# adaLN rows paced anew beside the second FFN matrix, activations split ahead of it, five plain blocks for seven in the last FFN

## The chip, the cores and the metric

One core of a Trainium2 chip. The metric is the device time of one execution in microseconds (us), the median of the runs shown. Everything is fp32; a product is made on TensorE from operands split into a high and a low part (hi·hi + hi·lo + lo·hi), so each product is three matmuls, and every weight that is loaded must first be split: ScalarE copies the rounded high part, VectorE subtracts it to get the low part.

## What is computed

Two layers; each is FFN half-step, mixer, FFN half-step, on 640 tokens (128 context, 512 latent). The rows `mod` (adaLN) are one vector-matrix product per conditioning vector (two of them) and per kind of row:

```python
def adaln(cvec, w_mod_l, b_mod_l):
    m = jax.nn.silu(cvec) @ w_mod_l + b_mod_l
    return m.reshape(cvec.shape[0], N_MOD, D_MODEL)

def swiglu(h, w1, w2):
    g, u = jnp.split(h @ w1, 2, axis=-1)
    return (jax.nn.silu(g) * u) @ w2

def ffn_half(x, mod, j, g_pre, g_post, w1, w2):
    h = modulate(rms_norm(x, g_pre), mod, j)
    return x + 0.5 * mod[:, j + 2][:, None, :] * rms_norm(swiglu(h, w1, w2), g_post)
```

with D_MODEL 1024 and D_FF 2816, that is 22 blocks of 128.

## The kernel before, in words

There are six stages: 0, 2, 3, 5 are FFNs, 1 and 4 are mixers. Tokens are held in two groups: A (two tiles of 128, width 256) and B (three tiles, width 384; the third is the context tile, number 4).

**First matrix.** Loop over 22 blocks f of D_FF. The first N_AONLY[s] blocks are run for group A alone, while VectorE, ScalarE and GpSimd finish the previous stage's boundary (norm, modulation, transposes) for group B. Then these blocks are run for group B; all but the last KEEP_F = 2 of them load and split their weights a second time for that. In stages 2, 3 and 5 (BLOCKS) the remaining blocks f are computed by `ffn1_blocks` (L651), which forms seven products of combined operands in place of eight plain ones; beside group B's plain blocks VectorE prepares the combined activations (`sums`, L612, then `sum_in_place`, L639). A pair of weight tiles of a block is loaded into the pool `tmp`, which has four buffers.

**Second matrix.** `ffn2` (L748) runs over the 22 blocks twice: a first pass for group A (22 x 2 x 2 x 3 = 264 matmuls of 512 columns) and a second pass for group B (396). The activations are split block by block, two blocks ahead (L765, L766). Results lie in PSUM banks fixed by tile (OB): tile 0 in banks 4 and 5, tile 1 in 6 and 7, tile 4 again in banks 4 and 5, so tile 4's matmuls of the second pass need tile 0's boundary to have read its banks. `second_pass` (L1364) lets the boundary of group A run at the head of the second pass.

**adaLN rows.** `ada` (L418) makes one row set per kind (G, S or T): eight loads of 512 KB of w_mod, for each of them two VectorE products with accumulation of 128x1024 (L436), one for each conditioning vector, then four matmuls with ones (L445) and, for G and S, one VectorE combination (L451, L453); the result is written to DRAM (L457) and loaded again, spread over all partitions, by `load_md` (L460). A row set is so 16 products at L436. The work is a generator that yields its estimated cost: 8 x (300 + 2 x 1150) + 1700 = 22500 ns a row set. `run` (L122) and `beside` (L137) advance it by a rate times the cost that the matmuls yield: 22 x 2 x 2 x 650 = 57200 ns in a first pass, 85800 ns in a second.

What is made where: stage 0 makes two stages' rows beside its first matrix, and ADA_LATE says which are made beside the second matrix: rows of stage 2 (three sets) in stage 0, rows of stage 3 (three) in stage 2, rows of stages 4 and 5 (three and one, as the last stage has no next) in stage 3, none in stage 5. The rate is ADA_RATE2 = 0.7 in both passes. The loads of `ada` are issued on SP's queue, in one line with the weight loads; their three buffers come free when L436 has read them.

The framework puts the instructions of each engine into a fixed order when the program is built, from their place in the program, their dependences and a cost model; `behind` moves the rows' instructions a little back in priority.

Of the kernel before, what the change touches and what calls it, by code (L numbers as in the profile page):

```python
# [8 lines left out]
F32 = mybir.dt.float32  # L9
F32R = mybir.dt.float32r  # L10
# [5 lines left out]
P = 128  # L16
D = 1024
KD = 8
FF = 2816
NF = 22  # L20
# [5 lines left out]
WA = 256  # L26
WB = 384
NEG = -1e30
OB = {0: (4, 5), 1: (6, 7), 2: (0, 1), 3: (2, 3), 4: (4, 5)}
N_AONLY = (7, 0, 5, 5, 0, 7)  # L30
ADA_LAG = 30
ADA_RATE = 0.65

ADA_LATE = {0: (2,), 2: (3,), 3: (4, 5), 5: ()}
ADA_RATE2 = 0.7

BLOCKS = (2, 3, 5)
S_LAG, S_RATE = 400, 0.45
# [112 lines left out]
def drain(*gens):  # L151
    for g in gens:
        for _ in g:
            pass
# [7 lines left out]
class Builder:  # L162
    def __init__(self, ctx, tc, a, n_stage=6):
        self.tc = tc
        self.nc = tc.nc
        self.a = a
        self.n_stage = n_stage
        pool = lambda name, bufs, **kw: ctx.enter_context(tc.tile_pool(name=name, bufs=bufs, **kw))
        self.c1 = pool("c1", 1)
        self.rawp = pool("raw", 5)  # L170
        self.wp = pool("wsp", 8)
        self.xp = pool("xp", 3)
        self.tmpp = pool("tmp", 4)
        self.stp = pool("st", 6)
        self.mdp = pool("md", 2)
        self.psp = pool("ps", 1, space=bass.MemoryType.PSUM)
        self.PS = self.psp.tile([P, 4096], F32, name="PS")
        self.ring = {}
        self.turn = {}
        self.drp = pool("dr", 1, space=bass.MemoryType.DRAM)  # L180
        self.xd = [self.drp.tile([P, D], F32, name=f"xd{t}", tag=f"xd{t}") for t in range(NT)]
        self.units = []
        self.plan()
        self.n_dma = 0
        self.n_split = 0
        self.n_use = 0
        self.dmas = []
        self.raws = {}
        self.spl = {}
        self.kept = {}  # L190
        self.pins = []
        self.lo_pool = 0
        self.xt = {}
        self.hT = {}
        self.md = {}
        self.rowd = {}
        self.pairs = {}
        self.gap = None
        self.kept_tmp = {}

    def bank(self, i):
# [498 lines left out]
    def mm_tok(self, key, tiles, order, stat, late=0, tail=1):  # L700
# [18 lines left out]
        while ci < n:  # L719
# [25 lines left out]
                    yield 650 * len(tiles)  # L745
            ci += 1

    def ffn2(self, l, i, g, last=False):  # L748
        wid = (WA, WB)[g]
        sp = {}  # L750

        order = list(range(NF))
        if g:
# [543 lines left out]
    def ffn_stage(self, s, l, i, pend):  # L1297
# [3 lines left out]
        na = N_AONLY[s]  # L1301
# [4 lines left out]
        with tc.tile_pool(name="gap", bufs=1, reuse_waits="tile") as gp, tc.tile_pool(name="actp", bufs=1, reuse_waits="tile") as ap, ExitStack() as late:  # L1306
# [19 lines left out]
            if s in BLOCKS:  # L1326
                with tc.tile_pool(name="sp", bufs=2, reuse_waits="tile") as sp:
                    self.sp = sp
                    self.SZ = [sp.tile([P, 4, 2 * WA + P], F32R, name=f"sz{n}", bufs=1) for n in range(2)]
                    self.S1 = [self.mdp.tile([P, D], F32, name=f"s1{n}", tag="mdG").bitcast(F32R).rearrange("p (k q) -> p k q", k=4) for n in range(2)]  # L1330
                    bg = behind(tc, self.sums(), S_LAG)
                    run(self.ffn1(l, i, fk + early[:-1], (1,)), (bg, S_RATE))
                    drain(bg)
                    self.load_pair(l, i, na)
                    run(self.ffn1(l, i, early[-1:], (1,)))
                    self.sum_in_place()
                    self.rings(acc=(0, 1, 2, 3, 4, 5, 6, 7))
                    run(self.ffn1_blocks(l, i, range(na, NF)))
            if s in BLOCKS:
                pools()  # L1340
            ada = lambda rows: behind(tc, self.ada(rows, block(self.wmp, "wmt"), block(self.accsp, "acc")), ADA_LAG)
# [12 lines left out]
                self.load_md(kind, s)  # L1354
            self.rings(ada=(3,))
            bg = ada(rows[1])
            run(self.ffn2(l, i, 0), (bg, ADA_RATE2))
            self.rings(ada=(7,))
            self.second_pass(s, last, self.ffn2(l, i, 1, last), bg)
            for t in (3, 4):  # L1360
# [3 lines left out]
    def second_pass(self, s, last, mm, bg=None):  # L1364
        q = STG[s]
        if bg:
            mm = beside(mm, bg, ADA_RATE2)
        b = self.boundary(s, GA, True, not last, 1, q["skew_a"])
        next(b)
        next(b)  # L1370
# [84 lines left out]
```

## Time and profile before

| | us |
|---|---|
| median of 3 runs | 2384.79 (2383.39 to 2386.68) |
| the profiled execution, device time | 2385.23 |
| its span in the trace | 2383.5 |
| stage 0, second matrix (first pass, second pass) | 66.57, 99.63 |
| stage 2, the same | 70.01, 97.57 |
| stage 3, the same | 69.11, 99.86 |
| stage 5, the same | 59.88, 89.56 |
| TensorE busy in the span | 2300.2 (97%) |
| VectorE busy in the span | 1827.1 (77%) |

A pass begins with its first matmul on the split activations and ends where the next one's begins. TensorE's busy time counts a matmul until its modelled end, so in the matmul stretches start-to-start times say more than the busy share: a stretch without gaps starts a 512-column matmul every 0.226 us.

### The profile page before, as it was taken

To read this page: it belongs to the slowest core of one execution; us is meant where nothing else is said; L and a number is where in the kernel's file an instruction comes from. 1 tells how busy PE (TensorE), PEld (TensorE's weight loads), DVE (VectorE), ACT (ScalarE), POOL (GpSimd) and SP (SyncE) were. 2 spreads that over 40 slices of the span, in tenths; PEclk is the share of its full clock that TensorE was granted. 3 is DMA by queue.
4 is the path that set the end of the run, shared out by engine and by line. 5 is a ranking of instruction groups with operands and counts; after the bars stand their busy time and mean duration, and the time that the engine had idled before them with its cause. 6 is when DMAs were issued, how large, how long until landed. Compare 5 with 4: busy or idle time off the path is not lost.

```text
span 2383.5 us, 37305 instructions
## 1 busy us (share of the span) xinstructions
PE 2300.2 (97%) x13304; PEld 2050.9 (86%) x13304; DVE 1827.1 (77%) x2914; ACT 1118.5 (47%) x2309; POOL 393.5 (17%) x432
## 2 busy tenths in 40 slices
PE   8999999999999999998999999999999989999998
PEld 6999897787778899996789999877777779999887
DVE  5568678977686788889976888899867674888754
ACT  5422224444776344454443444444555553444543
POOL 2000000305324200000240000020645360000000
PEclk9999999999999999999999999999999999999999
DMA  9457657644325522247653322667621354232542
GB/s 295 117 174 244 200 189 261 232 157 137 98 72 168 160 85 84 80 160 248 222 181 120 89 86 75 212 227 244 204 74 63 106 173 134 75 89 71 187 158 93
DMA packets 330481, 360.07 MB, mean 151 GB/s; under 512 B 20451, under 2 KB 239843, under 8 KB 330294
## 3 DMA queue, kind: packets, MB, share of 16 engines
q1 hardware_dynamic: 326694, 344.58, 45.5%
q10 hardware_dynamic: 3600, 13.11, 1.4%
q8 instruction: 104, 1.70, 0.3%
q14 instruction: 83, 0.68, 0.1%
HBM read 341.50 MB, written 16.12 MB: 150 GB/s over the span
## 4 chain that ended last, share of the span: by engine, by line
PE 71%; DVE 13%; DMA 6%; issue 5%; POOL 2%; ACT 2%; SPq 1%; DVEq 0%; ACTq 0%; POOLq 0%
PE PS L366 69%; DVE wlo L331 3%; DMA wmt<-in_w_mod 3%; DVE acc L436 3%; DMA raw<-in_ffn_w 2%; DVE alo L766 1%; PE PS L445 1%; POOL tmp L520 1%; DVE ast L1063 1%; DVE x L509 1%; PE PS L1086 1%; DVE tl L362 1%; DVE h1lo L362 1%; POOL wlo L331 1%; ACT whi L329 0%
## 5 line engine op out<-in xcount | busy, mean ns | idle before, releaser
L329 ACT ACTIVATE whi<-raw 128x512 fp32r<-128x512 f32 x668 | 416.5, 630 | 525.5 <-PE PS L366 379.5
L331 DVE TENSOR_TENSOR wlo<-raw,whi 128x512 fp32r<-128x512 f32 x614 | 455.2, 755 | 198.7 <-ACT whi L329 190.0
L366 PE MATMUL PS<-whi,ahi 128*128 128x512 f32 x920 | 353.6, 392 | 0.0
L366 PE MATMUL PS<-h1hi,whi 128*128 128x384 f32 (+1 forms) x1016 | 341.5, 337 | 6.4 <-ACT h1hi L361 6.4
L366 PE MATMUL PS<-h1lo,whi 128*128 128x384 f32 (+1 forms) x1016 | 344.6, 339 | 0.0
L366 PE MATMUL PS<-wlo,ahi 128*128 128x512 f32 x880 | 342.7, 391 | 0.0
L366 PE MATMUL PS<-h1hi,wlo 128*128 128x384 f32 (+1 forms) x1016 | 341.8, 336 | 0.0
L329 ACT ACTIVATE whi<-tmp 128x512 fp32r<-128x512 f32 x294 | 185.7, 633 | 244.6 <-PE PS L366 175.3
L436 DVE SCALAR_TENSOR_TENSOR acc<-wmt,ccs,acc 128x1024 f32<-128x1024 f32 x224 | 279.9, 1279 | 26.8 <-DMA wmt<-in_w_mod 26.7
L366 PE MATMUL PS<-h0hi,whi 128*128 128x256 f32 x1016 | 287.3, 284 | 7.6 <-DVE act L602 7.4
L366 PE MATMUL PS<-whi,alo 128*128 128x512 f32 x840 | 272.7, 395 | 21.2 <-DVE alo L766 20.9
L366 PE MATMUL PS<-h0hi,wlo 128*128 128x256 f32 x1016 | 285.4, 282 | 0.0
L366 PE MATMUL PS<-h0lo,whi 128*128 128x256 f32 x1016 | 285.3, 281 | 0.0
L331 DVE TENSOR_TENSOR wlo<-tmp,whi 128x512 fp32r<-128x512 f32 x294 | 201.7, 687 | 77.5 <-ACT whi L329 71.4
L366 PEld LDWEIGHTS PS<-whi,alo 128*128 128x128 f32 x840 | 155.3, 188 | 66.6 <-DVE alo L766 30.0
L366 PEld LDWEIGHTS PS<-h0hi,whi 128*128 128x128 f32 x1016 | 193.5, 191 | 18.4 <-DVE act L602 8.8
L366 PEld LDWEIGHTS PS<-whi,ahi 128*128 128x128 f32 x920 | 173.8, 189 | 39.1 <-ACT ahi L765 1.7
L366 PE MATMUL PS<-sz,whi 128*128 128x384 f32 x784 | 199.3, 335 | 0.0
L366 PEld LDWEIGHTS PS<-h0hi,wlo 128*128 128x128 f32 x1016 | 193.6, 191 | 4.3 <-issue 3.4
L366 PEld LDWEIGHTS PS<-h1hi,whi 128*128 128x128 f32 x1016 | 190.7, 188 | 7.0 <-ACT h1hi L361 7.0
L366 PEld LDWEIGHTS PS<-wlo,ahi 128*128 128x128 f32 x880 | 166.2, 189 | 34.7
L366 PEld LDWEIGHTS PS<-h0lo,whi 128*128 128x128 f32 x1016 | 193.9, 191 | 1.8 <-issue 1.7
(239 smaller groups left out, 4204.6 us busy)
## 6 DMA issues: line engine op xcount, KB each, us to landing
raw<-in_ffn_w SPq DMA_DIRECT2D x540, 256.0 KB
wmt<-in_w_mod SPq DMA_DIRECT2D x136, 512.0 KB
tmp<-in_ffn_w SPq DMA_DIRECT2D x98, 512.0 KB
raw<-in_w_in SPq DMA_DIRECT2D x80, 256.0 KB
xd<-x ACTq DMA_DIRECT2D x25, 512.0 KB
x<-xd SPq DMA_DIRECT2D x25, 512.0 KB
raw<-in_w_out SPq DMA_DIRECT2D x64, 128.0 KB
mdG<-rowG SPq DMA_DIRECT2D x12, 512.0 KB
```

What stands on the lines that cost most here:

```text
L329: self.nc.scalar.activation(hi, r, AF.Copy)
L331: eng.tensor_tensor(lo, r, hi.bitcast(F32), ALU.subtract)
L362: i1 = (eng or self.nc.vector).tensor_tensor(lo, src, hi.bitcast(F32), ALU.subtract)
L366: self.nc.tensor.matmul(out, w, m, start=start, stop=stop)
L436: nc.vector.scalar_tensor_tensor(accs[s], w, self.cc[:, s, k:k + 1], prev, ALU.mult, ALU.add)
L445: nc.tensor.matmul(ps[32 * q:32 * q + 32, :], self.ones[:, 0:32], accs[q // 2][:, 512 * (q % 2):512 * (q % 2) + 512], start=True, stop=Tru ...
L509: nc.vector.scalar_tensor_tensor(x, tmp, r, x, ALU.mult, ALU.add)
L520: nc.gpsimd.tensor_tensor(tmp[:, hs], tmp[:, hs], self.md["T", st][:, hs], ALU.add)
L766: self.nc.vector.tensor_tensor(lo, a, hi[:, 0:wid].bitcast(F32), ALU.subtract)
L1063: nc.vector.tensor_reduce(mx, S, AX.X, ALU.max)
L1086: nc.tensor.transpose(ps[:, w * c + P * j:w * c + P * j + P], pt[:, n * j + P * (c0 + c):n * j + P * (c0 + c) + P], self.ident)
```

## The change

The rates become a pair for each stage (first pass, second pass): 0.3 and 0.62 in stages 0, 2 and 3, 0.5 and 0.62 in stage 5. Stage 5's one row set moves from stage 3 to stage 5's own first pass; what is left of it is issued behind that pass, and the loading of the row follows there. Before the last combined block of the first matrix the activations of blocks 0 and 1 for group A are split into one buffer of the pool `tmp`, and the first pass starts with them. In stage 5 five blocks in place of seven are plain, so two more go through `ffn1_blocks`.

```diff
-N_AONLY = (7, 0, 5, 5, 0, 7)
+N_AONLY = (7, 0, 5, 5, 0, 5)
-ADA_LATE = {0: (2,), 2: (3,), 3: (4, 5), 5: ()}
-ADA_RATE2 = 0.7
+ADA_LATE = {0: (2,), 2: (3,), 3: (4,), 5: (5,)}
+ADA_RATES = {0: (0.3, 0.62), 2: (0.3, 0.62), 3: (0.3, 0.62), 5: (0.5, 0.62)}
+    def split_first(self):
+
+        t = self.tmpp.tile([P, D], F32, name="first", tag="tmp").bitcast(F32R)
+        self.early = {}
+        for f in range(2):
+            hi, lo = (t[:, 512 * f + WA * n:512 * f + WA * n + WA] for n in range(2))
+            self.split(hi, lo, self.act[f, 0])
+            self.early[f] = (hi, lo)
     def ffn2(self, l, i, g, last=False):
         sp = {}
+        if g == 0 and self.early:
+            sp, self.early = self.early, {}
-                    run(self.ffn1_blocks(l, i, range(na, NF)))
+                    run(self.ffn1_blocks(l, i, range(na, NF - 1)))
+                    self.split_first()
+                    run(self.ffn1_blocks(l, i, range(NF - 1, NF)))
-            run(self.ffn2(l, i, 0), (bg, ADA_RATE2))
+            run(self.ffn2(l, i, 0), (bg, ADA_RATES[s][0]))
+            if last:
+                drain(bg)
+                self.load_md("G", s)
     def second_pass(self, s, last, mm, bg=None):
-            mm = beside(mm, bg, ADA_RATE2)
+            mm = beside(mm, bg, ADA_RATES[s][1])
```

## Rows read from the trace of the kernel before

**Rows 1.** Windows, eight passes: busy (xcount) of PE, PEld, DVE, ACT, POOL; PEclk, DMA share, GB/s.
```profile
364.30:430.87 66.57, 63.26 (x274) 49.42 (x273) 60.05 (x84) 30.29 (x58) 0.95 (x1) 1.00 0.79 261
430.87:530.50 99.63, 97.08 (x429) 77.14 (x428) 82.43 (x105) 46.53 (x88) 20.05 (x16) 0.98 0.56 185
1054.37:1124.38 70.01, 63.48 (x273) 49.36 (x273) 63.39 (x90) 31.03 (x59) 0.95 (x1) 1.00 0.83 281
1124.38:1221.95 97.57, 94.69 (x429) 75.75 (x428) 80.40 (x103) 45.86 (x88) 16.57 (x15) 1.00 0.58 188
1515.58:1584.69 69.11, 63.90 (x273) 49.36 (x273) 61.25 (x88) 30.82 (x59) 0.96 (x1) 1.00 0.83 286
1584.69:1684.55 99.86, 97.26 (x429) 77.02 (x428) 97.55 (x118) 46.70 (x88) 21.72 (x16) 0.98 0.68 227
2227.21:2287.09 59.88, 59.88 (x265) 49.57 (x265) 39.45 (x68) 32.77 (x66) 0.86 (x2) 1.00 0.60 198
2287.09:2376.65 89.56, 89.56 (x397) 74.16 (x395) 43.78 (x69) 35.16 (x68) 2.59 (x6) 1.00 0.35 118
```

**Rows 2.** Groups, TensorE, first pass of stage 3: busy, mean ns | idle before, releaser.
```profile
L366 PE MATMUL PS<-whi,alo 128*128 128x512 f32 x79 | 23.3, 400 | 4.7 <-DVE alo L766 4.7
```

**Rows 3.** Windows of line L436 alone (VectorE busy), four of the passes.
```profile
430.87:530.50 99.63, 29.81 (x24) 0.98 0.56 185
1124.38:1221.95 97.57, 28.06 (x23) 1.00 0.58 188
1515.58:1584.69 69.11, 30.05 (x25) 1.00 0.83 286
1584.69:1684.55 99.86, 48.76 (x39) 0.98 0.68 227
```

**Rows 4.** Groups, VectorE, first pass of stage 3.
```profile
L436 DVE SCALAR_TENSOR_TENSOR acc<-wmt,ccs,acc 128x1024 f32<-128x1024 f32 x21 | 26.2, 1281 | 5.4 <-DMA wmt<-in_w_mod 5.3
...
L453 DVE SCALAR_TENSOR_TENSOR wmt<-PS,wmt 128x512 f32<-128x512 f32 x1 | 0.7, 685 | 0.0
```

**Rows 5.** Timeline, TensorE, end of stage 0: the four matmuls of a row set.
```profile
495.55 1.07 PE L445 MATMUL PS<-acc,ones 128*32 128x512 f32 x8
```

**Rows 6.** Timeline, VectorE and GpSimd, boundary in stage 0's second pass.
```profile
454.64 3.47 DVE L331 TENSOR_TENSOR wlo<-raw,whi 128x512 fp32r<-128x512 f32 x2
...
452.35 6.88 POOL L520 TENSOR_TENSOR tmp<-tmp,mdT 128x512 f32<-128x512 f32 x4
```

**Rows 7.** Windows, a stretch at half clock in stage 0's second pass.
```profile
461.00:464.40 3.40, 3.40 (x10) 2.62 (x9) 3.40 (x6) 1.49 (x3) 0.00 (x0) 0.50 0.46 138
```

**Rows 8.** Windows of line L366 alone (PE, PEld), 15 us behind stages 0 and 3.
```profile
530.50:545.50 15.00, 11.46 (x51) 9.11 (x50) 1.00 0.74 246
1684.50:1699.50 15.00, 12.24 (x50) 8.78 (x48) 1.00 0.62 207
```

**Rows 9.** Windows, stage 5: group B plain, combined blocks, group A plain.
```profile
1990.00:2030.00 40.00, 40.00 (x229) 40.00 (x228) 17.94 (x28) 13.88 (x25) 0.00 (x0) 1.00 0.38 113
2050.00:2200.00 150.00, 150.00 (x1012) 150.00 (x1011) 130.52 (x243) 72.40 (x144) 0.00 (x0) 1.00 0.29 85
...
1972.00:1983.00 11.00, 11.00 (x95) 11.00 (x95) 5.42 (x10) 2.92 (x5) 0.00 (x0) 1.00 0.75 215
```

**Rows 10.** Opening of stages 3 and 5 to group B's first matmul: windows; its wait.
```profile
1222.17:1252.63 30.46, 25.28 (x205) 23.95 (x204) 28.85 (x29) 17.04 (x36) 25.26 (x21) 1.00 0.72 225
1926.68:1961.45 34.77, 27.55 (x217) 26.46 (x215) 31.93 (x31) 21.90 (x43) 31.12 (x25) 0.95 0.53 160
...
L366 PE MATMUL PS<-h1hi,whi 128*128 128x384 f32 x2 | 0.6, 390 | 2.5 <-ACT h1hi L361 2.5
```

**Rows 11.** Chain of work, stage 3: start, us, what.
```profile
1549.35 6.27 DMA wmt<-in_w_mod
...
1604.57 4.11 DMA rowS<-wmt
```

**Rows 12.** Timeline, VectorE, end of stage 5's first pass: tile 0's boundary.
```profile
2282.57 0.69 DVE L499 TENSOR_TENSOR tmp<-PS,mdG 128x512 f32<-128x512 f32 x1 [4.72 <-ACT mk L498]
```

More of the change, by code (lines that the diff above doesn't have):

```diff
@@ L746, in mm_tok @@
             ci += 1
+    def split_first(self):
+        t = self.tmpp.tile([P, D], F32, name="first", tag="tmp").bitcast(F32R)
+        self.early = {}
+        for f in range(2):
+            hi, lo = (t[:, 512 * f + WA * n:512 * f + WA * n + WA] for n in range(2))
+            self.split(hi, lo, self.act[f, 0])
+            self.early[f] = (hi, lo)
     def ffn2(self, l, i, g, last=False):
```

## The prediction, made before the change was run

> **What bounds the kernel now.** I began with the windows of the eight passes over the second matrix, because the change works mainly there. Stage 5's passes make no adaLN rows, so they are the control: the first pass takes 59.88 us and the second 89.56, with TensorE busy in all of both [rows 1]. Stages 0, 2 and 3 have the same matmuls and take 66.57, 70.01 and 69.11 in the first pass and 99.63, 97.57 and 99.86 in the second [rows 1]. Together that is 502.75 against 3 x 149.44 = 448.3 us: 54.4 us are spent on the rows and on the boundary. In the first pass VectorE is busy 60.05 to 63.39 us of 67 to 70 [rows 1], and TensorE's idle time sits before matmuls that wait for the low part of the activations, which VectorE makes (4.7 us in stage 3) [rows 2]. About half of VectorE's load there is the rows' products (30.05 us in 25 instructions) [rows 3]. VectorE itself waits for the rows' loads, 5.4 us [rows 4], with the DMA engines at 0.79 to 0.83 of their time; stage 5 runs at 0.60 [rows 1]. So the first passes are overfed with rows. The second passes of stages 0 and 2 have VectorE 17 us free, that of stage 3 has almost none (97.55 of 99.86) [rows 1].
>
> Of the 54.4 us not all can be won. Each row set costs TensorE about 1.07 us of its own matmuls [rows 5], so some 3.2 a stage, and the boundary's 16 transposes (two tiles, eight each) at most 1.9, estimated at the 11/95 us of a 256-column start [rows 9]. About 54.4 - 3 x 5.2 = 39 us is the most that pacing could give.
>
> **The first passes of stages 0, 2, 3.** At rate 0.7 the plan puts 0.7 x 57.2 = 40.0 of the rows' cost units there, at 0.3 it puts 17.2, which at 2.6 a step is 6.6 steps or 13 products at L436, where the trace has 25 [rows 3]. One product takes 1.28 us [rows 4]. Without rows VectorE's load in stage 3 is 61.25 - 30.05 - 0.7 = 30.5 us [rows 1, 3, 4], by stage 5's row at most 39.45 [rows 1]; with 13 x 1.28 = 16.6 it comes to 47 to 56 of 60 us. DMA traffic falls by 12/2 x 0.52 = 3.1 MB a pass. TensorE then becomes the bound, and the row set's matmuls move to the second pass. I take 60.5 us each (59.88 and a little): 205.69 - 181.5 = **-24.2**. Bounds: -26 if nothing is left over; -13 if the loss falls only as the number of products does.
>
> **The second passes.** All three now carry 48 - 13 = 35 products, against 24, 23 and 39 [rows 3]. One is 48.76/39 = 1.25 us of busy time. VectorE's load becomes 82.43 - 29.81 + 43.75 + 0.7 = 97.1 us in stage 0, 80.40 - 28.06 + 44.5 = 96.8 in stage 2 and 97.55 - 48.76 + 44.5 = 93.3 in stage 3 [rows 1, 3, 4]. TensorE needs 89.56 + 3 x 1.07 + 2 = 94.8 [rows 1, 5]. Stage 3 shows how well a saturated VectorE is used: 97.55 of 99.86, 0.977 [rows 1]. So stages 0 and 2 come out at 97.1/0.977 = 99.4 and 99.1, and stage 3 at TensorE's 94.8 and the boundary's stall, 97.5. Against 99.63, 97.57 and 99.86 this is -0.2, +1.5 and -2.4, in all **-1.1**. Bounds: 95 each (-12), and +11 if the durations do not overlap at all, about 104, 103 and 101.
>
> What the boundary costs at the head of this pass stays. While GpSimd adds the shift (four instructions, 6.88 us), two splits of VectorE take 3.47 us [rows 6] where another instruction of 512 columns takes 0.69 [rows 4], and in stage 0 a stretch at half clock (granted 0.50, the 1.2 GHz level, 10 matmuls in 3.40 us) follows [rows 7], worth 1.7 us. That stretch may go or come, which I put into the range.
>
> The Trainium skill, "SBUF — State Buffer", "Who interferes with whom", states that a VectorE instruction with two SBUF inputs and a GpSimd instruction that reads SBUF exclude each other for the whole instruction. This trace agrees (3.47 us for two splits under GpSimd's adds). The rule speaks against carrying more rows in the second pass, as their products have two such inputs.
>
> **Openings behind the second passes.** The plan's remaining 67.5 - 17.2 = 50.3 units at 0.62 use 81 of 85.8, so the rows end at 94% of the pass and, with VectorE full, run into the next stage by some us. Stage 3 does that already with its fourth set. In the 15 us behind stage 0, where the rows ended early, 51 projection matmuls start, and behind stage 3, where they run over, 50 [rows 8]: an overrun is worth little. Queued behind a late load on SP are the mixer's small loads and the spread rows. I take +1 for stages 1 and 3 each, and -1 for stage 4: **+1** in all, from -3 to +6.
>
> **Two more combined blocks in stage 5.** A combined block has 7 x 12 = 84 matmuls at 150/1012 us, 12.45 us; a plain one 48 for group A at 11/95 and 48 for B at 40/229, 5.56 + 8.38 = 13.94 [rows 9]. Two of them give **-3.0**. The two are early blocks, whose weights were loaded and split twice; the saved loads were hidden anyway. The cover is what matters: group A's plain blocks hide group B's boundary, and 2 x 5.56 = 11.1 us of it go. But in the trace TensorE has run only 217 matmuls (24 of them transposes, so about four blocks of 48) when it stops 2.5 us for group B [rows 10]; the five blocks that remain are 240. Stage 3 does the same with five, in 30.46 us [rows 10]. So I take no loss; the bounds are +11 (all the cover missed) and -4 more (if the opening becomes like stage 3's, 34.77 - 30.46).
>
> **Stage 5's own row set.** 16 products and a combination, 21.2 us of VectorE, come beside a first pass with 39.45 us busy: 60.6 of 60 on paper, somewhat less as starts overlap. TensorE pays 1.07 [rows 5]. At 0.5 the plan ends at 45 of 57.2. The row's last product then comes near 45 us, and stage 3 was four products, or two steps of 2.6, behind its plan of 29 (25 done) [rows 3], so it comes near 50; writing the row takes 4.11, a 512 KB load 6.27 [rows 11]. The row lies ready at about 61 to 62. In the trace VectorE reads tile 0's banks 4.5 us before the pass ends [rows 12], but tile 4 needs these banks only after 12 matmuls, about 2.7 us into the second pass, at 63. Two reads of 0.69 must fit between. I take 1.07 + 1 = **+2**, from +1 to +8 (VectorE's queue stands behind the waiting read, splits included).
>
> **Early split.** It takes two low parts from the head of a pass and puts them beside a combined block, where VectorE is busy 130.52 of 150 us [rows 9]. The buffer comes free with block 20's weights. Before the change TensorE already passes from one matrix to the other without a gap (stage 5: busy throughout [rows 1]). **0**, from -2 to +1.
>
> Sum: -24.2 - 1.1 + 1 - 3.0 + 2 + 0 = -25.3 us. The profiled execution took 2385.23 (span 2383.5 and 1.7 around it), 0.44 over the median; 2384.79 - 25.3 = 2359.5, so **2360 us**.
>
> **Rivals.** (1) The second passes give part of it back: VectorE's durations do not overlap, +11 in place of -1.1. Sum -13, **2372 us**. Against it: stage 3 carried 39 products in 99.86 us. The same time comes out if the first passes are bound by loads more than by VectorE (-13). (2) Slower: a saturated second pass. VectorE falls behind from the boundary on, the waiting products hold the rows' buffers, SP waits with the weight loads behind them. For the three passes: +11 for durations end to end and up to four products in each held by GpSimd's adds, 3.47/2 - 0.69 = 1.05 us each [rows 4, 6], +13, and the openings at +6, stage 5's row at +8: -24.2 + 24 + 6 + 8 - 3 = +11, **2396 us**. It decides from some 107 us a second pass, if the rest comes as forecast. By the skill's rule named above the products would be held so; the trace has 97.55 us of VectorE in 99.86 without it. (3) The rate does not move what is executed: the built order follows VectorE's own backlog and not the plan, so the first pass keeps 25 products; only the blocks' -3, the moved set in stage 3 (-2.4) and in stage 5 (+2) count, **2381 us**. Against it: 25 products of the 29 planned did run in the first pass, so the order follows the plan [rows 3].
>
> **How the numbers follow.** Forecast 0.62, rival 1 with both its causes 0.22, rival 3 with its neighbourhood 0.09, rival 2 0.07. The range takes the forecast's own bounds (2346 if the second passes reach 95 and stage 5 opens like stage 3) and rival 1: 2346 to 2376. A measurement here tells about 0.2%, 4.8 us, from no change. Faster 0.86, same 0.08, slower 0.06.
>
> **What would show it.** Right: first passes of stages 0, 2, 3 at 60 to 62 us with 11 to 14 products and no wait for the low part; second passes at 97 to 100 with VectorE over 93 busy; stage 5's first matrix 3 us shorter, its second 1 to 4 longer. Wrong: first passes still over 64, or second passes over 103, or TensorE idle for several us at the head of stage 5's second pass.

## The result, and the profile after

The changed kernel takes 2398.7 us (median of 6 runs, 2394.73 to 2404.24), the kernel before, beside it, 2384.27 (2381.71 to 2387.58): a ratio of 1.0063, 95% interval 1.0046 to 1.0080. The forecast was 2360, in a range of 2346 to 2376; the kernel became slower by 0.6%. The profiled execution took 2399.27 us (span 2397.5), 14.0 more than that of before.

The windows of the eight passes answer [rows 1] (columns as there):

```profile
365.76:434.08 68.32, 63.28 (x266) 50.32 (x265) 46.52 (x72) 31.46 (x65) 0.00 (x0) 0.98 0.59 199
434.08:532.06 97.98, 95.96 (x428) 75.65 (x427) 90.13 (x111) 42.80 (x81) 17.28 (x15) 1.00 0.66 222
1067.74:1137.34 69.60, 63.63 (x265) 50.22 (x265) 47.35 (x74) 30.68 (x63) 0.00 (x0) 0.98 0.66 231
1137.34:1239.10 101.76, 99.50 (x437) 77.01 (x436) 96.82 (x118) 44.04 (x82) 17.23 (x16) 0.98 0.65 216
1531.84:1599.90 68.06, 63.14 (x266) 50.28 (x266) 46.05 (x72) 30.54 (x63) 0.00 (x0) 0.97 0.65 226
1599.90:1701.20 101.30, 98.31 (x429) 77.71 (x428) 91.85 (x112) 42.87 (x80) 15.83 (x15) 0.97 0.65 221
2237.67:2300.00 62.33, 62.33 (x273) 49.66 (x273) 50.92 (x77) 30.91 (x63) 0.87 (x2) 1.00 0.79 256
2300.00:2390.75 90.75, 90.31 (x397) 73.92 (x395) 46.87 (x75) 35.28 (x68) 2.59 (x6) 1.00 0.38 127
```

In the first passes of stages 0, 2 and 3 VectorE fell from 60 to 63 us of work to 46 or 47, as the plan wanted, and the DMA share from about 0.8 to 0.6. The passes did not become shorter: 205.98 us against 205.69 in all. The engine that was thought to be the bound is now a third idle, and TensorE has as many gaps as before. What VectorE waits for stands in its groups of stage 0's first pass (busy, mean ns of one | idle before, releaser), with TensorE's group that waits:

```profile
L332 DVE TENSOR_TENSOR wlo<-raw,whi 128x512 fp32r<-128x512 f32 x37 | 24.6, 686 | 3.0 <-ACT whi L330 3.0
L437 DVE SCALAR_TENSOR_TENSOR acc<-wmt,ccs,acc 128x1024 f32<-128x1024 f32 x12 | 14.9, 1281 | 18.0 <-DMA wmt<-in_w_mod 18.0
...
L367 PE MATMUL PS<-wlo,ahi 128*128 128x512 f32 x88 | 35.5, 404 | 5.0 <-DVE wlo L332 5.0
```

SP's waits in the same stretch (line, what it waits for: us in total, times, longest):

```profile
SPq L284 <- DVE alo L778: 26.1, 15, 6.6
SPq L284 <- DVE wlo L332: 24.9, 17, 5.9
```

Before the products (L437, the old L436) VectorE stands idle for 18.0 us, always for a load of w_mod. In the same pass of the kernel before it was 5.7:

```profile
L436 DVE SCALAR_TENSOR_TENSOR acc<-wmt,ccs,acc 128x1024 f32<-128x1024 f32 x21 | 26.2, 1281 | 5.7 <-DMA wmt<-in_w_mod 5.7
```

VectorE's timeline after the change shows one such place:

```profile
387.42 0.69 DVE L332 TENSOR_TENSOR wlo<-raw,whi 128x512 fp32r<-128x512 f32 x1
391.61 2.48 DVE L437 SCALAR_TENSOR_TENSOR acc<-wmt,ccs,acc 128x1024 f32<-128x1024 f32 x2 [3.50 <-DMA wmt<-in_w_mod]
394.01 0.68 DVE L332 TENSOR_TENSOR wlo<-raw,whi 128x512 fp32r<-128x512 f32 x1
```

From 388.1 to 391.6 VectorE does nothing, with two products at the head of its order and the weights' low parts behind them. Each split that is late keeps a raw weight buffer, and SP's next weight load (L284) waits for it: 51.0 us in the two rows above and up to 6.6 at a time, where the same two rows of the kernel before have 34.2 and at most 3.4. And so TensorE waits for low parts of weights (5.0 us) in place of those of activations [rows 2].

The second loss lies behind the second passes. Windows of L437 alone (VectorE busy) in stage 0's second pass and behind it, and windows of the projections' line L367 alone (PE, PEld), 15 us and 30 us behind the same pass; the first of these two answers [rows 8]:

```profile
434.08:532.06 97.98, 40.38 (x32) 1.00 0.66 222
532.06:545.50 13.44, 3.86 (x4) 0.89 0.65 200
...
532.06:547.06 15.00, 9.38 (x33) 6.70 (x32) 0.85 0.69 223
...
532.06:562.06 30.00, 19.90 (x68) 13.54 (x66) 0.89 0.57 179
```

Three products start behind the pass, in the mixer, the last of them 8.5 us behind it (8.6 in stage 3); the fourth of the window is the end of one from the pass. In 15 us 33 projection matmuls start where there were 51 [rows 8], in 30 us 68 where the kernel before has 98, in its window of the same line:

```profile
530.50:560.50 30.00, 23.84 (x98) 17.54 (x96) 1.00 0.65 212
```

Counted from the first projection matmul, the 30th starts 7.7 us later than in the kernel before and the 98th 10.7 later; by the first FFN matmul it is 13.1. VectorE's timeline at this place shows the products standing between the steps of group B's boundary (L500, L510), and ScalarE's next step of that boundary waiting for it:

```profile
532.00 1.88 DVE L500 TENSOR_TENSOR tmp<-PS,mdG 128x512 f32<-128x512 f32 x3
533.79 1.28 DVE L437 SCALAR_TENSOR_TENSOR acc<-wmt,ccs,acc 128x1024 f32<-128x1024 f32 x1
534.98 1.29 DVE L500 TENSOR_TENSOR tmp<-PS,mdG 128x512 f32<-128x512 f32 x2
...
537.00 1.28 DVE L437 SCALAR_TENSOR_TENSOR acc<-wmt,ccs,acc 128x1024 f32<-128x1024 f32 x1
...
539.39 1.28 DVE L510 SCALAR_TENSOR_TENSOR x<-tmp,r,x 128x1024 f32<-128x1024 f32 x1
...
540.71 1.06 ACT L513 ACTIVATE tmp<-x 128x1024 f32<-128x1024 f32 x1 [6.41 <-DVE x L510]
```

Group B's first L510 starts 7.3 us behind the pass. In the kernel before the same step (L509) starts 0.2 us ahead of the pass's end (530.50), in VectorE's timeline:

```profile
530.28 1.27 DVE L509 SCALAR_TENSOR_TENSOR x<-tmp,r,x 128x1024 f32<-128x1024 f32 x1
```

A table by stage, from start to start in the profiled executions; a mixer is counted from the end of the second pass to the first FFN matmul behind it.

| us | before | after | difference |
|---|---|---|---|
| ahead of stage 0's second matrix | 364.3 | 365.8 | +1.5 |
| first passes 0, 2, 3 | 205.69 | 205.98 | +0.3 |
| second passes 0, 2, 3 | 297.06 | 301.04 | +4.0 |
| stage 1 (mixer) | 230.3 | 243.4 | +13.1 |
| stage 4 (mixer) | 241.9 | 243.5 | +1.6 |
| first matrix, stages 2 and 3 | 586.8 | 584.6 | -2.2 |
| first matrix, stage 5 | 300.5 | 292.8 | -7.7 |
| second matrix, stage 5 | 149.44 | 153.08 | +3.6 |

These add to 14.2 of the 14.0 us. (Here and in the windows a second pass ends with the start of its last matmul; where a run below has no window shown, with the start of the next one, 0.2 us later.)

Each column is one profiled execution, and its rows vary by themselves. The run below with five plain blocks in stage 5 and nothing else has, in stages 0 to 3, the same instructions in the same order on every engine as the kernel before, and yet its first passes add to 202.6 us, its second passes to 300.6, and its stage 1 takes 234.1. So the +0.3 and the +4.0 of the passes are no more than an unchanged order shows. Stage 1's +13.1 lies clear of that, and so do the two rows of stage 5, whose second matrix took 149.4 us in each of the three profiles without a row set there.

### The profile page after: what moved, and what is told of

It is laid out like the page before. It is cut to its first block, busy times and chain, and to the rows that moved or that the text cites. A ratio compares the mean times of both kernels' runs of the same rounds, so it can differ in the third digit from the quotient of the medians.

```text
span 2397.5 us, 37273 instructions
## 1 busy us (share of the span) xinstructions
PE 2312.0 (96%) x13280; PEld 2056.0 (86%) x13280; DVE 1838.6 (77%) x2938; ACT 1113.2 (46%) x2313; POOL 373.7 (16%) x428
## 4 chain that ended last, share of the span: by engine, by line
PE 73%; DVE 10%; DMA 7%; issue 4%; ACT 3%; POOL 2%; SPq 0%; DVEq 0%; ACTq 0%; POOLq 0%
PE PS L367 70%; DMA raw<-in_ffn_w 5%; DVE wlo L332 3%; DVE acc L437 2%; DMA wmt<-in_w_mod 1%; PE PS L446 1%; ACT whi L330 1%; POOL tmp L521 1%; DVE ast L1075 1%; DVE alo L778 1%; PE PS L1098 1%; PE PS L529 1%; ACT pt L1081 0%; DMA raw<-in_w_in 0%; DVE tl L363 0%
## 5 line engine op out<-in xcount | busy, mean ns | idle before, releaser
L330 ACT ACTIVATE whi<-raw 128x512 fp32r<-128x512 f32 x652 | 406.6, 629 | 572.3 <-PE PS L367 397.1
L332 DVE TENSOR_TENSOR wlo<-raw,whi 128x512 fp32r<-128x512 f32 x602 | 447.6, 756 | 176.7 <-ACT whi L330 168.2
L367 PE MATMUL PS<-wlo,ahi 128*128 128x512 f32 x856 | 338.7, 396 | 15.7 <-DVE wlo L332 15.7
L367 PE MATMUL PS<-whi,ahi 128*128 128x512 f32 x884 | 345.1, 398 | 7.7 <-DVE tmp L500 7.2
L367 PE MATMUL PS<-h1lo,whi 128*128 128x384 f32 (+1 forms) x1000 | 339.3, 339 | 0.8 <-DVE h1lo L363 0.8
L367 PE MATMUL PS<-h1hi,wlo 128*128 128x384 f32 (+1 forms) x1000 | 336.5, 336 | 0.0
L367 PE MATMUL PS<-h1hi,whi 128*128 128x384 f32 (+1 forms) x1000 | 334.9, 336 | 0.4 <-ACT h1hi L362 0.4
L437 DVE SCALAR_TENSOR_TENSOR acc<-wmt,ccs,acc 128x1024 f32<-128x1024 f32 x224 | 280.7, 1282 | 62.3 <-DMA wmt<-in_w_mod 62.1
L367 PE MATMUL PS<-whi,alo 128*128 128x512 f32 x828 | 317.6, 395 | 0.2 <-DVE alo L778 0.2
L330 ACT ACTIVATE whi<-tmp 128x512 fp32r<-128x512 f32 x306 | 193.3, 633 | 251.5 <-PE PS L367 182.5
L367 PE MATMUL PS<-h0hi,whi 128*128 128x256 f32 x1000 | 282.9, 284 | 8.7 <-DVE act L603 4.6
L367 PE MATMUL PS<-h0hi,wlo 128*128 128x256 f32 x1000 | 281.1, 282 | 0.2 <-DVE wlo L332 0.2
L367 PE MATMUL PS<-h0lo,whi 128*128 128x256 f32 x1000 | 281.1, 281 | 0.0
L332 DVE TENSOR_TENSOR wlo<-tmp,whi 128x512 fp32r<-128x512 f32 x306 | 209.9, 687 | 78.7 <-ACT whi L330 72.6
L425 POOL MEMSET wmt<- 128x1024 f32 x16 | 15.3, 956 | 1402.6 <-PE PS L367 784.3
L367 PEld LDWEIGHTS PS<-whi,ahi 128*128 128x128 f32 x884 | 169.0, 191 | 48.8 <-DVE tmp L500 10.7
L367 PEld LDWEIGHTS PS<-wlo,ahi 128*128 128x128 f32 x856 | 162.6, 190 | 55.8 <-DVE wlo L332 21.9
L367 PE MATMUL PS<-sz,whi 128*128 128x384 f32 x816 | 207.4, 335 | 0.0
L367 PEld LDWEIGHTS PS<-h0hi,whi 128*128 128x128 f32 x1000 | 190.7, 191 | 18.6 <-DVE act L603 5.2
L367 PEld LDWEIGHTS PS<-h0hi,wlo 128*128 128x128 f32 x1000 | 190.9, 191 | 4.7 <-issue 3.4
L367 PEld LDWEIGHTS PS<-h0lo,whi 128*128 128x128 f32 x1000 | 191.1, 191 | 1.9 <-issue 1.7
L367 PEld LDWEIGHTS PS<-whi,alo 128*128 128x128 f32 x828 | 156.6, 189 | 41.5 <-issue 5.9
```

The source lines that it names most:

```text
L330: self.nc.scalar.activation(hi, r, AF.Copy)
L332: eng.tensor_tensor(lo, r, hi.bitcast(F32), ALU.subtract)
L367: self.nc.tensor.matmul(out, w, m, start=start, stop=stop)
L425: nc.gpsimd.memset(wb, 0.0)
L437: nc.vector.scalar_tensor_tensor(accs[s], w, self.cc[:, s, k:k + 1], prev, ALU.mult, ALU.add)
```

## The experiments

Each kernel ran beside the kernel before, whose median was 2382.3 to 2386.3 us in these sessions. Ratios are to it, with the 95% interval.

**Parts of the change.** Only the rates back:

```diff
-ADA_RATES = {0: (0.3, 0.62), 2: (0.3, 0.62), 3: (0.3, 0.62), 5: (0.5, 0.62)}
+ADA_RATES = {0: (0.7, 0.7), 2: (0.7, 0.7), 3: (0.7, 0.7), 5: (0.5, 0.62)}
```

> The changed kernel with the rates of stages 0, 2 and 3 back at 0.7 in both passes; the moved row set, the early split and the two combined blocks stay. Theory (waits): the low rate costs in two places, in the first passes by VectorE standing behind products whose load has not landed, and at the opening of stage 1 by rows that run over. With the old rates both go: VectorE's wait for the rows' loads in stage 0's first pass falls from 18.0 to about 6 us, stage 1 is 230 us long again in place of 243, stage 5 keeps its gain. 2377 us (2372 to 2382), 22 us under the changed kernel. Rival (blocks or split): the rates are neutral, and the early split or the other block count upset the order of the instructions: then it stays at 2395 to 2403.

Measured 2377.71 us, ratio 0.9973 (0.9963 to 0.9983). The new rates alone cost 21 us in the changed kernel. No product stands behind a second pass here; stage 1 takes 231.6 us and stage 4 234.8, 11.8 and 8.7 less than after. First passes 66.5, 66.3 and 66.9, in all 6.3 less than after, second 100.1, 103.1 and 101.5, in all 3.0 more. By these two profiles most of the 21 us lies in the mixers.

The kernel before with five plain blocks in stage 5 and nothing else (`N_AONLY` ending in 5):

> The kernel before with five in place of seven plain blocks in stage 5 and nothing else. By the prediction's step -3.0 us: 2381. By what the changed kernel's trace shows (stage 5's first matrix 292.6 us in place of 300.4) -7.7 us: 2377. If the group B boundary were uncovered: over 2384.

Measured 2378.28, ratio 0.9976 (0.9966 to 0.9985): -5.7 us by the medians; stage 5's first matrix 292.8 us, as in the changed kernel. The kernel before with the early split alone:

> The kernel before with the early split in stages 2, 3 and 5 and nothing else. Prediction's step: 0, from -2 to +1: 2382 to 2386. Rival: the split reorders the start of the first pass (the changed kernel's trace waits for the low part of the weights there, the kernel before's for the low part of the activations): a change of over 4 us either way.

Measured 2384.98, ratio 1.0006 (0.9997 to 1.0015): nothing, though in its one profile the first passes of stages 2 and 3 are 3.1 and 2.4 us shorter and their second passes 5.4 and 2.2 longer.

**Loads in time.** The changed kernel with every load of a row set issued one step ahead:

```diff
+            load(0)
             for k in range(KD):
-                w = wt()
-                with self.after(self.gate_dma):
-                    nc.sync.dma_start(w, src[:, k, :])
+                if k + 1 < KD:
+                    load(k + 1)
+                w = ws.pop(k)
```

> The changed kernel, rates as changed, but each load of the rows' weights is issued one step (two products) earlier; loads, products and rates are the same in number. Theory (waits): VectorE no longer stands before the products in the first passes (18.0 us in stage 0 falls under 5), the first passes of stages 0, 2 and 3 fall from 68.3, 69.6 and 68.1 to 61 to 63, and the overrun into stage 1 shrinks: 2370 to 2384 us. Rival (load): what costs is the amount of VectorE work and of DMA traffic in the passes, which is the same here: 2395 to 2403 us, first passes within 1.5 us of the changed kernel's.

Measured 2373.23, ratio 0.9955 (0.9943 to 0.9967). First passes 65.4, 61.9 and 63.7, with 14, 16 and 16 products (14, 14 and 12 after); two of the three lie above the theory's 61 to 63, and in stage 0 VectorE still waits 11.0 us for loads. In stage 5 the early loads fell among the x tile loads at the head of the pass: 67.5 us. So the same without stage 5:

> The changed kernel with each load one step ahead in stages 0, 2 and 3 and as changed in stage 5. With the loads ahead everywhere (2373 us) stage 5's first pass took 67.5 us against 62.3, its second row load being issued among the tile loads at the head of the pass. Theory (the head of the pass has no room in the transfers): stage 5's first pass is 62 to 63 again, the others stay at 62 to 65: 2366 to 2371 us. Rival (67.5 was another order of the instructions, not the early loads): 2371 to 2376 us.

Measured 2369.68, ratio 0.9942 (0.9924 to 0.9960); stage 5's first pass 63.0, those of the others 64.5, 64.4 and 64.0, where VectorE still waited 9.2, 7.6 and 7.4 us for loads. Two steps ahead:

```diff
+                for j in (k + 1, k + 2)[:1 + (k > 0)]:
+                    if ahead and j < KD and j not in ws:
+                        load(j)
```

> The changed kernel (0.3 and 0.62) with the loads of a row set issued two steps ahead in stages 0, 2 and 3, in place of one step (2369.68 us, first passes 64.5, 64.4 and 64.0 us, where VectorE still waited 8 us for loads). Theory (VectorE's waits for loads are what is left of the first pass's loss): these waits fall below 4 us and the first passes come to 61 to 62; 2360 to 2366 us. Rival (two loads in flight take the DMA engines from the weights, or all three row buffers are held): waits for raw weights take their place, the first passes stay at 64 or more; 2369 to 2378 us.

Measured 2357.20, ratio 0.9889 (0.9874 to 0.9903), below the theory's range. VectorE's products in stage 3's first pass, in the changed kernel:

```profile
L437 DVE SCALAR_TENSOR_TENSOR acc<-wmt,ccs,acc 128x1024 f32<-128x1024 f32 x10 | 12.4, 1281 | 13.4 <-DMA wmt<-in_w_mod 13.4
```

The same group with loads one step ahead (the run without stage 5):

```profile
L447 DVE SCALAR_TENSOR_TENSOR acc<-wmt,ccs,acc 128x1024 f32<-128x1024 f32 x14 | 17.4, 1280 | 7.4 <-DMA wmt<-in_w_mod 7.4
```

The same group with loads two steps ahead:

```profile
L448 DVE SCALAR_TENSOR_TENSOR acc<-wmt,ccs,acc 128x1024 f32<-128x1024 f32 x14 | 17.5, 1280 | 3.5 <-DMA wmt<-in_w_mod 3.5
```

And the window of that pass with two steps (all engines, as [rows 1]):

```profile
1502.05:1562.35 60.30, 60.27 (x265) 49.36 (x265) 52.26 (x80) 30.97 (x63) 1.91 (x3) 1.00 0.80 269
```

With 16 products in the pass in place of 12 (each row set's first two stand in a group of their own) and this wait down from 13.4 us to 7.4 and 3.5, the pass goes from 68.1 to 64.0 and 60.3, where TensorE has next to no gap. Stage 2 came to 60.0, stage 0 to 63.8. One pass in one profile varies by 2 us or so, but the profiles of all runs in this document agree: at rate 0.3 the first passes of stages 0, 2 and 3 took 68.1 to 70.5 us with each load in its own step (12 passes, mean 69.4), 61.9 to 65.4 with one step (6, mean 64.0) and 60.0 to 63.8 with two (9, mean 61.1). At the old rate with each load in its own step they took 66.0 to 70.0 (12, mean 67.3).

Are loads in time enough, at the old rates? One step ahead with 0.7, with and without stage 5:

> The changed kernel with the rates of stages 0, 2 and 3 at 0.7 and each load one step ahead (all stages). Theory (waits): at the old rates VectorE stood only some 6 us a pass before the rows' products, so the early loads give at most 2 to 4 us a pass, and stage 5 loses 5 as it did with the loads ahead: 2372 to 2380 us against 2377.7 with the old rates alone. If the early load helps at any rate as it did at the low one (25 us): 2355 us.

> The changed kernel with the old rates of 0.7 in stages 0, 2 and 3 and each load of a row set issued one step ahead in those stages, not in stage 5. Against the run with 0.3 and 0.62 and the same loads (2369.68 us) the rates are the only edit. Theory (overruns and late loads are the whole cost; a low rate is worth something only if its loads come in time and its rows end inside the pass): first passes 66 to 67 us in place of 64.3, stage 4 near 235 in place of 245, stage 5's first pass 63 in place of the 67.0 that it had with loads ahead; the time is 2368.99 - 4 = 2363 to 2367 us. Rival (with loads in time the low rate is the better one by its first passes): 2370 to 2374.

Measured 2368.99, ratio 0.9940 (0.9924 to 0.9956), 3 us under its theory's range, and 2366.74, ratio 0.9937 (0.9921 to 0.9953), inside it. Stage 3's first pass of the second:

```profile
L447 DVE SCALAR_TENSOR_TENSOR acc<-wmt,ccs,acc 128x1024 f32<-128x1024 f32 x23 | 29.3, 1280 | 0.0
...
L367 PE MATMUL PS<-whi,alo 128*128 128x512 f32 x75 | 24.5, 396 | 2.6 <-DVE alo L788 2.6
```

Here VectorE never waits for a load, yet the pass takes 66.8 us: with 27 products it is full (63.9 us busy), and TensorE waits for it. So both are needed for 60 us: few products, and their loads in time.

**Does the rate itself space the products?** The loads of the row sets cut to one of eight in stages 0, 2 and 3's second matrix, the products left:

> The changed kernel with only the first of eight weight loads of each row set that is made beside the second matrix of stages 0, 2 and 3; all eight steps' products read that one buffer, so these rows are not the reference's. The products, their places and the rates stay. Theory (waits for loads): the first passes fall to 60 to 63 us, VectorE's wait for the rows' loads under 5 us, stage 1 about 235: 2362 to 2376 us. Rival (VectorE's amount of work, with the boundary, sets the passes): first passes stay within 2 us of 68, 2393 to 2401 us.

Measured 2365.10, ratio 0.9925 (0.9908 to 0.9943). The total came out as the theory said, but the first passes stayed at 66.1, 67.1 and 66.5, the rival's figure. Windows of the products' line alone (VectorE busy) in stage 0's first pass tell why:

```profile
363.90:378.00 14.10, 7.59 (x6) 1.00 0.44 137
378.00:392.00 14.00, 8.06 (x7) 1.00 0.52 167
392.00:406.00 14.00, 4.70 (x4) 1.00 0.53 168
406.00:420.00 14.00, 0.00 (x0) 1.00 0.67 202
```

All products ran in the first 42 us (an instruction across a border counts in both windows), and TensorE lost 4.7 us of the pass to late low parts of the activations. Without loads to wait for, the products run as early as VectorE's order lets them; in the changed kernel they are spread from 368.7 to 433.9, so what had spaced them were the loads. This run is therefore no clean test of the loads; the two above are.

**Rows that run over into the mixers.** The second rate 0.9 in stage 0 alone, then in stages 0 and 3, everything else as changed:

> The changed kernel with one number changed: stage 0's second-pass rate 0.9 in place of 0.62, so that its rows end before the pass does. Theory (overrun): stage 1's 13 us come from the three products and two row sets' matmuls that run behind the pass; without them stage 1 takes 230 to 235 us in place of 243, its first group B projection comes 44 us after the pass in place of 54, the second pass is at most 3 us longer: 2386 to 2391 us. Rival (the mixer's order of instructions changed with the rest, the overrun only goes along): 2395 to 2403 us, stage 1 still 241 or more.

> The changed kernel with the second rate 0.9 in place of 0.62 in stages 0 and 3 (one edit more than the run that did it in stage 0 alone, 2396.02 us), so that in both the rows should end inside the second pass. Theory (rows that run over into a mixer cost it 9 to 12 us): stage 1 to its first FFN matmul again near 232 us, and stage 4, 243.5 in the changed kernel and 234.8 in the one with the old rates, falls to about 235 to 237; the time is 2396 - 7 = 2386 to 2391 us. Rival (an overrun costs a mixer little in itself, and what is won at its opening is lost in the second pass before it): stage 4 stays above 241, or the second pass of stage 3 grows from 101.5 to 108; the time stays at 2394 to 2400.

Measured 2396.02, ratio 1.0048 (1.0031 to 1.0066), and 2392.10, ratio 1.0034 (1.0022 to 1.0046). No product runs over any more where the rate is 0.9. Stage 1 fell to 232.3 and 233.6, as the theory said, stage 4 in the second run to 238.5, where it said 235 to 237. But the medians lie 5 and 1 us above the theory's ranges: stage 0's second pass grew from 98.2 to 102.0 in both runs, that of stage 3 from 101.5 to 103.6. In the second run 5.8 us of the 14.7 that the mixers won were so lost; stage 3's part of it is uncertain, as its pass took 99.3 us in the first run with its rate unchanged.

With loads one step ahead and rates of 0.45 and 0.75:

> Loads one step ahead in stages 0, 2 and 3, rates 0.45 and 0.75 there in place of 0.3 and 0.62, so the plan ends inside the second pass (0.45 x 57.2 + 0.75 x 85.8 = 90.1 units of 67.5 wanted). Theory (overrun into the mixers costs, the spacing in the first pass gains if loads come in time): first passes 64 to 66 us, no product behind a second pass, stages 1 and 4 at 232 and 235; 2358 to 2366 us, the shortest of all. Rival (the rate moves time only between the two passes; the mixers' openings vary for other reasons): stage 4 at 240 or more, 2366 to 2374 us.

Measured 2369.08, ratio 0.9942 (0.9930 to 0.9955), the rival's figure, though not by its mechanism: no product over, stage 4 at 236.0 and stage 1 at 233.3, but second passes of 105.2, 100.8 and 101.2 (99.1, 100.6 and 95.4 with 0.3 and 0.62), and first passes of 61.1, 65.2 and 65.6. At one step ahead the middle rates won nothing in all.

By which way does an overrun cost? One candidate was SP's queue: the row's write (L458) waits there for its result, with the mixer's weight loads behind it. The write of the last set (kind T) moved to ScalarE's queue, in the changed kernel and in the kernel with loads two steps ahead:

```diff
-                nc.sync.dma_start(dst[q // 2:q // 2 + 1,
+                (nc.scalar if kind == "T" else nc.sync).dma_start(dst[q // 2:q // 2 + 1,
```

> The changed kernel with one edit: the write of the last row set's result to DRAM (kind T) is issued on ScalarE's queue in place of SP's. Its products still run over into the mixers. Theory (the write waits for the last product, and the mixer's weight loads stand behind it on SP, which in the changed kernel pauses its w_in loads from 540.6 to 548.7 us): the pause goes, stage 1 to its first FFN matmul falls from 243.4 to about 236 and stage 4 from 243.5 to about 237; 2384 to 2392 us. Rival (the overrunning products and matmuls hold VectorE and TensorE in themselves, queue or not): both stages stay above 241; 2395 to 2401 us.

> Loads two steps ahead in stages 0, 2 and 3 at the changed kernel's rates (2357.2 us), with the write of kind T issued on ScalarE's queue in place of SP's; one product a stage still runs over. Theory (the queue is what the mixers pay for): stage 4 falls from 245.3 to 236 to 238 and stage 1 from 236.1 to 232 to 234; 2344 to 2351 us. Rival (the engines' own share): stage 4 above 241; 2354 to 2360 us.

Measured 2394.85, ratio 1.0040 (1.0026 to 1.0053), with stage 1 at 241.0 and stage 4 at 243.0; and 2363.18, ratio 0.9904 (0.9891 to 0.9918), with stage 4 at 248.7. The first lies at the rival's figure, the second above both. The theory of the queue found no support. SP's weight loads paused even without the write (first run, the same place):

```profile
537.61 0.85 SPq L284 DMA_DIRECT2D raw<-in_w_in  x2
543.60 0.33 SPq L791 DMA_DIRECT2D nsink<-in_attn_sink  x1
```

The engines' own orders show at the head of stage 4 in the second run, ScalarE and then TensorE:

```profile
1665.06 0.60 ACT L461 ACTIVATE wmt<-PS 128x512 f32<-128x512 f32 x1 [5.31 <-issue]
...
1663.91 1.05 PE L457 MATMUL PS<-acc,ones 128*32 128x512 f32 x4
1665.71 0.50 PE L367 MATMUL PS<-whi,h0hi 128*128 128x512 f32 x1 [0.75 <-ACT wmt L461]
```

ScalarE stood 5.3 us before its copy of the row (L461), which needs the row's matmuls (L457). The profile names no releaser here, but the last of those matmuls came at 1663.9, behind 22 projection matmuls in TensorE's order, and ended 0.1 us before the copy. Behind the copy are the high parts and the next step of group B's boundary (L524). A single product behind the pass is enough for this, and the write's queue is not the reason for this wait: the run with the same loads and the write on SP has it too:

```profile
1665.09 0.60 ACT L461 ACTIVATE wmt<-PS 128x512 f32<-128x512 f32 x1 [5.46 <-issue]
```

The other way round, the overrun taken away with loads two steps ahead, by a second rate of 0.72 in stages 0 and 3:

> Loads two steps ahead in stages 0, 2 and 3 (2357.2 us) and the second rate 0.72 in place of 0.62 in stages 0 and 3, so that the plan ends at 84% of the pass and no product stands behind it. Theory (one product and its row write behind the pass cost stage 4 about 10 us and stage 1 about 4): stage 1 at 232, stage 4 at 235, second passes 1 to 3 us longer; 2344 to 2352 us. Rival (stage 4's 245 us with loads ahead are not the overrun's): stage 4 stays above 241; 2354 to 2362 us.

Measured 2349.10, ratio 0.9852 (0.9836 to 0.9867), in the theory's range and the best of all: 1.5% below the kernel before. Windows of its first and second passes in stage 3, and 30 us of projections behind them (L367 alone):

```profile
1498.87:1559.26 60.39, 60.27 (x265) 49.34 (x265) 52.42 (x80) 31.21 (x63) 1.88 (x3) 1.00 0.78 268
1559.26:1656.70 97.44, 97.44 (x436) 76.13 (x435) 89.83 (x111) 43.03 (x83) 12.95 (x14) 1.00 0.69 225
...
1656.70:1686.70 30.00, 23.20 (x98) 17.80 (x96) 1.00 0.65 208
```

First passes 61.2, 60.7 and 60.4; second 97.5, 98.7 and 97.4; stage 4 at 233.8 in place of 245.3, stage 1 at 234.1 in place of 236.1. The row's copy no longer stands in ScalarE's order there, and L524 starts 2.1 us behind stage 3's second pass, with the overrun 10.6:

```profile
1658.83 1.05 ACT L524 ACTIVATE tmp<-x 128x1024 f32<-128x1024 f32 x1
```

All 17 profiles together show what an overrun goes with. Stage 1 took 230.3 to 235.8 us where no product started behind the pass (11 profiles, mean 233.0), 235.4 to 236.1 with one (4) and 241.0 and 243.4 with three. Stage 4 took 233.8 to 238.5 with none (7), 239.9 to 248.7 with one (7) and 241.3 to 243.5 with three (3).

The head of the mixer is not all of it. In the kernel before, stage 4's 250th projection matmul comes only 0.8 us later than in the best run, the 430th 9.7 later. The traces also show that the order of the instructions changes with the overrun, far into the stage. In five of the seven profiles without one, stage 4's order is the same on all four engines; with one product over (two steps ahead, 0.62) 683 of its 1192 matmuls stand at the same place in TensorE's order as in those. The move of the write alone does as much: between the two runs with loads two steps ahead, write on SP and write on ScalarE, 441 of 1192 keep their place. So the runs show that an overrun goes with a longer mixer; no run separates the overrunning instructions from the other order that is built around them, and the runs with the moved write are no clean test of the queue.

## Why the prediction was wrong, point by point

**The first passes** (-24.2 forecast, +0.3 measured) are the step that failed. The count of products (13 forecast, 14, 14 and 12 seen), VectorE's load (47 to 56, seen 46 to 47) and the fall of the DMA traffic were right. Wrong was "TensorE then becomes the bound". I had read VectorE's 5.4 us of waiting for loads [rows 4] as part of overfeeding, which would go with the number of products. It grew instead: over all products of a pass from 5.7, 6.6 and 7.7 us in stages 0, 2 and 3 to 18.0, 17.1 and 15.4, since each product stands at a fixed place in VectorE's order, its load is issued only in its own step, and nothing else may pass it. Even the +0.3 flatters the change: by the means over all profiles the low rate alone made each first pass 2.1 us longer (69.4 for 67.3). The fix of the loads alone, at the same rates, gave 60.0 to 63.8 us and so the forecast's 60.5: the mechanism of VectorE's load was real, but it was one of two limits. Rival 1 named the loads as a cause and kept half of the gain; in fact nothing was left. Rival 3 (the order does not follow the plan) is out, as the products did move.

**The second passes** (-1.1 forecast, +4.0 measured) came to 98.0, 101.8 and 101.3 us for 99.4, 99.1 and 97.5, in all within the bounds (stage 3's at its upper one, 101), and no further off than profiles of one order differ. What the traces do show is new: TensorE waits 2.0, 2.3 and 3.0 us at their head for tile 0's step L500, between whose instructions products stand in VectorE's order, where the kernel before has no such wait, and half clock follows (granted 0.57, mostly the 1.2 GHz level, in the 4 us from 1143 in stage 2). With loads in time they came to 95.0 to 98.7. Rival 2 wanted 107 us; no run reached it, and the slower result came another way. By the rule of the Trainium skill that the rival named ("SBUF — State Buffer", "Who interferes with whom") GpSimd's adds could have held products; in stage 0's second pass the products took 40.38 us in 32 instructions, 1.26 each, so none of weight was held. But this does not test the rule: in none of the three second passes did a product run beside these adds. One that ran beside a GpSimd split of 1.30 us behind stage 3's second pass (at 1702.90) took 2.03 us in place of 1.28.

**The openings** (+1 forecast, +13.1 for stage 1 and +1.6 for stage 4 measured) are the second step that failed: "an overrun is worth little". It rested on 51 and 50 matmuls in 15 us [rows 8], and that window was both too short and taken behind an overrun of a single product. The kernel before already paid: its stage 4 takes 241.9 us, with the same rate and no overrun 234.8. So the forecast of -1 for stage 4 missed 7 us that could be had, and +1 for stage 1 missed some 10 that could be lost (243.4 against the mean of 233.0 without an overrun). The named victims, loads behind a late load on SP, were not seen to be it: with the write moved away the loss stayed. That products, row matmuls and copy hold the boundary up in the engines' orders is seen in the waits at L513 and L461; how the loss divides among them, the half clock behind them (granted 0.85 to 0.90 in the 15 us) and the other order of the rest of the mixer stays open.

**Two more combined blocks** (-3.0 forecast, -7.7 in the profile, -5.7 by the medians of the run alone). The term was mis-sized by its own lower bound. After, stage 5's opening, group B's plain blocks and the combined blocks take, in this order:

```profile
1944.89:1978.05 33.16, 28.29 (x217) 27.40 (x216) 30.20 (x31) 20.76 (x40) 28.53 (x23) 0.90 0.53 164
1978.05:2025.64 47.59, 47.59 (x290) 47.59 (x289) 28.59 (x46) 18.25 (x31) 0.00 (x0) 1.00 0.40 117
2025.64:2237.67 212.03, 212.03 (x1429) 212.03 (x1429) 181.46 (x338) 103.39 (x209) 0.96 (x1) 1.00 0.28 83
```

The opening took 34.77 before [rows 10], the plain blocks behind it 78.57 and the combined ones 187.19. The combined blocks cost +24.8, as worked out (2 x 12.45). The opening and the plain ones gave 1.6 + 31.0 = 32.6, where 27.9 were counted. So 4.7 us more went with the blocks, close to the -4 that I had put only into the bounds. In the kernel before TensorE waits 2.5 us at the end of the opening [rows 10] and 0.8 behind it, and a stretch at half clock follows (granted 0.50 from 1962.8 to 1966.1); after, the window of the plain blocks has no wait and a granted clock of 1.00.

**Stage 5's own row set** (+2 forecast, +3.6 measured): +2.5 in the first pass and +1.2 in the second, inside the bounds. The row came late as feared; the read of tile 0's banks, at 2282.57 before [rows 12], stood behind the row's loading until here:

```profile
2301.28 1.29 DVE L500 TENSOR_TENSOR tmp<-PS,mdG 128x512 f32<-128x512 f32 x2 [6.42 <-DMA mdG<-rowG]
```

TensorE lost 0.4 us to it at the head of the second pass, waiting for a high part of the activations. **The early split** cost and gave nothing, as forecast.

By its own list of signs the forecast was wrong at the first: first passes over 64 us.

## What to carry to other kernels

An engine that is busy 90% of a stage is not shown to be its only limit: before its load is thinned out, look at what each of its instructions waits for, because in a fixed order one instruction that waits for a just-issued load holds everything behind it, however idle the engine has become. Background work is worth pacing only if its loads are issued well ahead (here two steps, 512 KB each) and its last step ends inside the stage that hides it: without either the pacing cost 21 us, the early loads then won 41 and the end inside the stage another 8. Against the old rates with loads one step ahead (2366.74 us; no run has them two steps ahead, but VectorE waited only 0 to 3 us a pass for loads there) the pacing was worth 18 in the end. An overrun must be priced over the whole of the next stage, not over its first microseconds. And one row of one profile is no measurement until a profile of the same order has shown how much it varies.

## What the runs showed of the hardware

I had not expected that fewer bytes and less work could leave a stage as long as it was: with DMA share 0.59 and VectorE at 46.5 of 68.3 us, TensorE's gaps were about those of before (15.9 us in the three first passes, 15.1 before). In the best kernel 16 products in place of 14 run in stage 0's pass of 61.2 us with the DMA engines at 0.69, so in this pass it was not the loads' bandwidth that held, but when they were issued. Moving a small write to another engine's queue had no sure use: 3.9 us less in the changed kernel, 6.0 more in the one with loads two steps ahead, with overlapping intervals of the ratios in both, and another order of the mixers. The Trainium skill, "Trainium Kernel Development and Optimization", under "Key Constraints", says that issuing DMAs from several engines saves only the sequencer's issue time, as all run on the same DMA engines; the two runs do not speak against it.
